# Sixteen experts, latent attention and gated attention of two transformer blocks: weight splits, tile order and pools

## The chip, the core and the metric

The kernel runs on one core of one Trainium2 chip. It has TensorE (PE: matrix products and transposes), VectorE (DVE), ScalarE (ACT), GpSimd (POOL) and a queue that issues transfers (SP); 16 DMA engines move data between memory and the core's on-chip buffer. Each engine runs its own instructions in order and waits for the others by semaphores. The metric is the time of one execution in device microseconds (us), the median of several runs.

## What is computed

Two blocks run one after the other on 1024 tokens of width 1024, all in fp32. The first has four mixers (latent attention, a pooling mixer, a state-space mixer, a gated recurrence), a feed-forward layer and an embedding layer. The second has gated linear attention and retention, then sixteen experts, each of which picks 128 tokens. The parts that matter here, shortened from the reference:

```python
def mla_mixer(c_q, c_kv, k_r, cos, sin, q_norm, w_uq, kv_norm, w_ukv):     # first block
    q = (rmsnorm(c_q, q_norm) @ w_uq).reshape(b, s, MLA_HEADS, QK_NOPE + QK_ROPE)      # 8 heads, 64 + 32
    q_nope, q_rope = q[..., :QK_NOPE], apply_rope(q[..., QK_NOPE:], cos, sin)
    kv = (rmsnorm(c_kv, kv_norm) @ w_ukv).reshape(b, s, MLA_HEADS, QK_NOPE + V_HEAD)   # 64 + 64
    k_nope, v = kv[..., :QK_NOPE], kv[..., QK_NOPE:]
    k_rope = apply_rope(k_r, cos, sin)                                                  # one for all heads
    # causal softmax of (q_nope k_nope + q_rope k_rope) * 96 ** -0.5, times v

def _token_mixer(...):                                                                  # second block
    # gated linear attention (4 heads, keys of 64) and retention (4 heads), forward and backward
    o_g = _head_rmsnorm(o_gf + _flip(o_gb), gla_norm_w) * jax.nn.silu(gg)
    o_r = _head_layernorm(o_rf + _flip(o_rb), ret_norm_w) * jax.nn.silu(rg)
    out = jnp.concatenate([o_g, o_r], axis=-1) @ w_out

def _expert_choice_ffn(h, w_router, w_gate, w_up, w_down):                              # second block
    aff = jax.nn.softmax((h @ w_router).astype(F32), axis=-1)
    gate, idx = lax.top_k(jnp.swapaxes(aff, 1, 2), cap)                                 # cap = 128
    xe = h[bidx, idx]
    a, u = xe @ w_gate, xe @ w_up                                                       # 1024 -> 1408
    ye = (silu(a) * u) @ w_down * gate[..., None]                                       # 1408 -> 1024
    return jnp.zeros_like(h).at[bidx, idx].add(ye)
```

## The kernel before

**Split matmuls.** Nearly every fp32 matrix product is done as three faster ones. `split` makes of a tensor its rounded high part on ScalarE (`_hi`) and the rest by a subtraction on VectorE (`_lo`); `mm3` then issues hi x hi, hi x lo and lo x hi into one accumulator (L104 to L106). A plain fp32 matmul does without the split and is two instructions in the trace. Accumulators and transposes share eight PSUM banks: `ps_mm` and `ps_ax` hand them out in turn, six and two of them in the expert stage.

**What sets the order.** The code is written as one sequential program; a scheduler of tiles places its instructions on each engine, which then runs its own in that order. Filler work covers the stages with long chains: `queue` holds generators (the gates' projections in the first block, the retention projections in the second) and `fill(n)` takes n pieces of them. `until(name)` takes pieces until one that is named is done. A pool (`tile_pool`) gives its space back when it is closed, so the pool that follows in the same space waits for the last readers of the first, stores among them.

**Latent attention** (`mla`, L507). The latents are held feature-major, split (`m_chi`, `m_clo`: 128 features x 1024 tokens each). For each of four groups of two heads, a loop over eight token tiles computes K and V token-major (`kv_tile`: 6 matmuls of 256 columns), then Q (`q_tile`: 9 matmuls of 192 columns). VectorE, ScalarE and GpSimd scale the rows and add the rotary part to `m_kx` (`rope`, four VectorE instructions); `turn` transposes each tile twice (`m_kt`, L607) into `m_kT` and `m_qT`. Scores, softmax and the product with V follow, with fillers between them.

**Gated attention** (`gla`, L1308) runs for two pairs of heads, each in a pool of its own. `decays` is a chain from a small matmul (`g_pre`) over ScalarE and VectorE to `g_la`; `states` transposes that (`g_ktp`, L1345) and builds the running states. Then come the scores (`g_s`), the outputs (`g_o`) and `head_out`. Ahead of the second pair the main program loads `qk` and `gv` anew.

**head_out** (L1078) normalizes a head's output and multiplies it by its gate (`ho_g`): a VectorE product with the row's factor, then a GpSimd product with the gate (L1094, L1095), then four transposes (`ho_p`, L1099). It serves gated attention and `retention`. The output projection behind retention runs its first accumulators in parts (k 0 to 4, 4 to 7, and the last, which needs retention's last head).

**Experts** (from L1822). `plan` lists the weight pieces in the order of use: gate of the next expert (8 pieces of 1408 columns), down of this one (8 of up to 1536), up of the next (8 of 1408). `begin(n)` starts the loads and splits of the first n pieces, `piece` asks for its own and `AHEAD` more. A piece is `split_piece` (load into `e_raw`, ScalarE conversion to `e_hi` at L1842, VectorE subtraction to `e_lo` at L1843) or `native_piece` (load into `e_nat`, used as plain fp32 at L1870), the latter for k = 3 and 7 of gate and up. The first expert uses plain pieces only (`first_piece`), which land in the buffers of the others. The loop over experts transposes the activations (`turn_act`: eleven transposes `e_at` at L2036, in three groups, each split to `e_ah` and `e_al`), computes the next expert's gate (`wide`), chooses and gathers a later expert's tokens (`choose`, `gather`, `turn_x` with `e_xt` and `e_xl`), computes `down`, and then the next expert's up. Its last VectorE product (L2026) ends the activations `e_act`. `last` adds the last expert's rows and normalizes.

## Time and profile before

| | us |
|---|---|
| median of 3 runs | 3755.38 (3750.97 to 3757.4) |
| profiled run | 3756.49 |
| its span | 3754.8 |
| TensorE busy | 3611.5 (96%) |
| VectorE busy | 2142.3 (57%) |
| ScalarE busy | 1630.4 (43%) |
| GpSimd busy | 575.5 (15%) |
| experts, from the second expert's start of transposes to the last down projection, 2944.0 to 3713.1 | 769.10 |

The page divides the span into 40 slices of about 94 us. An engine that is nearly always busy sets the time; for the others it counts when they make that one wait. The timeline shows the start of an instruction, its duration, and in brackets how long its engine had stood idle and which instruction ended that. Matmuls overlap, so what one of them costs is the time from its start to the next one's start, not its duration. The windows give the busy time of each engine in a stretch, the granted clock of TensorE, the share of time in which the DMA engines were busy and the rate in GB/s.

### The profile page before, as it was taken

The numbers are of one execution on the slowest core, as the hardware profiler recorded it, in microseconds if no ns is written. First come the engines' busy times: TensorE is split into PE (matmuls) and PEld (weight loads), VectorE is DVE, ScalarE is ACT, GpSimd is POOL, SyncE is SP. The second block draws the span as 40 slices with busy tenths as digits, with TensorE's granted clock in tenths as the row PEclk, the third lists the DMA queues.
The fourth block names the chain that finished last, engine by engine and source line by source line (L and its number), as shares of the span: only waits on it lengthen the run. The fifth ranks groups of instructions, "written<-read, shape, count | busy, mean of one in ns | idle before, by whom it ended". The sixth has DMA issues, their size and how long they took to land. (4 is left out here: it accounts for less than half of the span.)

```text
span 3754.8 us, 47815 instructions
## 1 busy us (share of the span) xinstructions
PE 3611.5 (96%) x18388; PEld 2917.8 (78%) x18388; DVE 2142.3 (57%) x3235; ACT 1630.4 (43%) x2393; POOL 575.5 (15%) x644
## 2 busy tenths in 40 slices
PE   8999999999999999999999999999996999999998
PEld 6787787777678788888888788778974677777776
DVE  5435424433556666555435647476544677777776
ACT  7433333333323322222125548445332566665565
POOL 0003311111132100000001201123321000123230
PEclk9999999999999999999999999999997999999999
DMA  4221211221456333233213342313356899999997
GB/s 127 65 63 54 79 52 49 74 65 65 144 193 195 109 97 106 91 100 96 73 45 101 105 116 68 96 56 128 119 195 240 286 353 364 358 341 347 373 348 263
DMA packets 295105, 581.84 MB, mean 155 GB/s; under 512 B 27246, under 2 KB 185036, under 8 KB 294876
## 3 DMA queue, kind: packets, MB, share of 16 engines
q1 hardware_dynamic: 272588, 508.47, 39.3%
q0 software_dynamic: 22288, 70.31, 5.6%
q8 instruction: 145, 2.38, 0.3%
q14 instruction: 84, 0.69, 0.1%
HBM read 512.61 MB, written 66.09 MB: 154 GB/s over the span
## 5 line engine op out<-in xcount | busy, mean ns | idle before, releaser
L104 PE MATMUL mm<-hh_hi,w_hi 128*128 128x512 f32 x1872 | 751.3, 402 | 6.2 <-ACT p_u L336 2.0
L105 PE MATMUL mm<-hh_lo,w_hi 128*128 128x512 f32 x1872 | 737.8, 394 | 0.2 <-DVE hh_lo L96 0.2
L106 PE MATMUL mm<-hh_hi,w_lo 128*128 128x512 f32 x1872 | 736.9, 394 | 0.5 <-DVE w_lo L96 0.5
L1843 DVE TENSOR_TENSOR e_lo<-e_raw,e_hi 128x1408 fp32r<-128x1408 f32 (+1 forms) x308 | 489.0, 1621 | 86.2 <-ACT e_hi L1842 70.8
L96 DVE TENSOR_TENSOR w_lo<-w_raw,w_hi 128x1024 fp32r<-128x1024 f32 (+4 forms) x278 | 352.2, 1283 | 278.2 <-ACT w_hi L94 276.8
L1842 ACT ACTIVATE e_hi<-e_raw 128x1408 fp32r<-128x1408 f32 (+1 forms) x308 | 415.2, 1389 | 124.0 <-PE mm L1868 78.7
L104 PEld LDWEIGHTS mm<-hh_hi,w_hi 128*128 128x128 f32 x1872 | 354.2, 189 | 91.1 <-issue 13.6
L94 ACT ACTIVATE w_hi<-w_raw 128x1024 fp32r<-128x1024 f32 (+4 forms) x278 | 270.4, 995 | 340.6 <-PE mm L105 189.8
L106 PEld LDWEIGHTS mm<-hh_hi,w_lo 128*128 128x128 f32 x1872 | 353.8, 189 | 78.4 <-issue 2.3
L105 PEld LDWEIGHTS mm<-hh_lo,w_hi 128*128 128x128 f32 x1872 | 354.2, 189 | 72.3 <-issue 4.9
L104 PE MATMUL mm<-w_hi,hh_hi 128*128 128x256 f32 (+1 forms) x896 | 291.0, 325 | 0.2 <-ACT w_hi L94 0.2
L105 PE MATMUL mm<-w_lo,hh_hi 128*128 128x256 f32 (+1 forms) x896 | 285.2, 318 | 0.0
L106 PE MATMUL mm<-w_hi,hh_lo 128*128 128x256 f32 (+1 forms) x896 | 283.9, 317 | 0.0
L1868 PE MATMUL mm<-e_hi,e_xl 128*128 128x512 f32 x540 | 203.6, 377 | 0.0
L1867 PE MATMUL mm<-e_lo,e_xh 128*128 128x512 f32 x540 | 202.7, 375 | 0.0
L105 PE MATMUL mm<-w_lo,a_hi 128*128 128x512 f32 x512 | 199.6, 390 | 0.0
L104 PE MATMUL mm<-w_hi,a_hi 128*128 128x512 f32 x512 | 199.6, 390 | 0.0
L106 PE MATMUL mm<-w_hi,a_lo 128*128 128x512 f32 x512 | 199.3, 389 | 0.0
L1866 PE MATMUL mm<-e_hi,e_xh 128*128 128x512 f32 x540 | 198.6, 401 | 0.0
L104 PEld LDWEIGHTS mm<-w_hi,hh_hi 128*128 128x128 f32 x896 | 172.5, 193 | 14.3 <-issue 0.8
L105 PEld LDWEIGHTS mm<-w_lo,hh_hi 128*128 128x128 f32 x896 | 172.7, 193 | 10.4 <-issue 1.0
L106 PEld LDWEIGHTS mm<-w_hi,hh_lo 128*128 128x128 f32 x896 | 172.5, 193 | 10.0
(658 smaller groups left out, 6325.4 us busy)
## 6 DMA issues: line engine op xcount, KB each, us to landing
e_raw<-in_w_exp_down_dram SPq DMA_DIRECT2D x112, 768.0 KB
e_raw<-in_w_exp_gate_dram SPq DMA_DIRECT2D x90, 704.0 KB
e_raw<-in_w_exp_up_dram SPq DMA_DIRECT2D x90, 704.0 KB
w_raw<-in_w_in_dram SPq DMA_DIRECT2D x82, 512.0 KB
w_raw<-in_w_ff_dram SPq DMA_DIRECT2D x64, 512.0 KB
w_raw<-in_w_ada_dram SPq DMA_DIRECT2D x48, 512.0 KB
e_nat<-in_w_exp_up_dram SPq DMA_DIRECT2D x32, 704.0 KB
e_nat<-in_w_exp_gate_dram SPq DMA_DIRECT2D x30, 704.0 KB
```

What stands on the lines that cost most here:

```text
L94: S.activation(hi, src, AF.Copy, scale=1.0 if scale is None else scale)
L96: V.tensor_sub(lo, src, hi.bitcast(F32))
L104: P.matmul(ps, ah, bh, start=start and k == 0, stop=False)
L105: P.matmul(ps, ah, bl, start=False, stop=False)
L106: P.matmul(ps, al, bh, start=False, stop=stop and k == nk - 1)
L1842: S.activation(hi[:, :n], r[:, :n], AF.Copy)
L1843: V.tensor_sub(lo[:, :n], r[:, :n], hi[:, :n].bitcast(F32))
L1866: P.matmul(ps, x[0][:, k], w[0][:, c0:c1], start=k == 0, stop=False)
L1867: P.matmul(ps, x[0][:, k], w[1][:, c0:c1], start=False, stop=False)
L1868: P.matmul(ps, x[1][:, k], w[0][:, c0:c1], start=False, stop=k == last)
```

## The change

**Experts.** Pieces 3 and 7 of gate and up are split like the others, for all experts from the second on; `native_piece` and the plain copies `e_xn` of the tokens are gone. The pools of `e_hi`, `e_lo` and `e_raw` have nine buffers each (7, 7 and 8 before, besides 3 of `e_nat`), and `AHEAD` is 8 in place of 6. The loads of all sixteen pieces of the first expert are issued ahead of the top-k, in program order, and `begin` is called during the first expert's gate too.

**Latent attention.** K and Q are computed feature-major at once, weights as the stationary side and 512 tokens as the moving one: K of two heads in 6 matmuls per half of the tokens, Q of one head in 9. V is computed for four heads at a time. The tables of the rotary angles (`m_trig`) and the rotated key part (`m_kpe`) are made and transposed once, by 16 transposes; the weights of Q are laid out so that rotated rows stand beside plain ones (`parted`). The row factor of Q moves into the softmax (`m_qs`), that of K into a row table (`m_krow`, two plain matmuls). `turn`, `rope` and `m_kx` are gone.

**Gated attention.** Both pairs use one pool. `gla` is a generator; the second pair's load and its first `decays` run from `following`, ahead of the first pair's last `g_o` and `head_out`.

**head_out** does both products in one VectorE instruction per 128 columns. **Retention's end** itself issues the output projection's parts k 0 to 4 and 4 to 7 for four tiles, ahead of the last transposes.

```diff
-    LO_A, N_LO, N_HI, N_RAW, N_NAT = 5, 7, 7, 8, 3
-    NATIVE = (3, 7)
-    AHEAD = 6
+    LO_A, N_LO, N_HI, N_RAW = 7, 9, 9, 9
+    AHEAD = 8
...
-        SP.dma_start(r[:, :n], src)
+        tc.keep_in_program_order(SP.dma_start(r[:, :n], src))
         return r
...
+    firsts = []
+    for which, name in enumerate(("w_exp_gate_2", "w_exp_up_2")):
+        src = I[name][0, 0].rearrange("(p j) n -> p j n", j=KD)
+        firsts += [first_piece(which * KD + k, src[:, k], 1408) for k in range(KD)]
...
-                split(x[0][:, b * 4:b * 4 + 3], x[1][:, b * 4:b * 4 + 3], t)
+                split(x[0][:, b * 4:b * 4 + 4], x[1][:, b * 4:b * 4 + 4], t)
...
-                made.append((native_piece if k in NATIVE else split_piece)(src[:, k], 1408))
+                made.append(split_piece(src[:, k], 1408))
...
-            if e == 0 and which == UP:
-                begin(k)
+            if e == 0:
+                begin(min(k, N_HI + N_LO - 2 * KD) if which == GATE else N_HI + N_LO - 2 * KD + k)
...
+            kT = mp2.tile([128, 2, T], F32, name="m_kT")
+            V.tensor_copy(kT[64:128, 0], kpe[64:128])
+            S.activation(kT[0:64, 1], kpe[0:64], AF.Copy)
...
+            def kv_weights(h0, n, s):
+                r = raw_half(2, n * 64)
+                for j in range(2):
+                    SP.dma_start(r[:, j].rearrange("p (h d) -> p h d", h=n), w_ukv[:, j, h0:h0 + n, s])
+                return parted(2, n * 64, r, [(0, 0, n * 64)])
+
             for hg in range(4):
...
+                w = kv_weights(hg * 2, 2, 0)
+                for h in range(2):
                     p = ps_mm()
...
+                    mm3(p, w, cT, 2, lambda t, k: t[:, k, :], lambda t, k: t[:, 3 + k, H5(h)])
+                    for x in range(2):
+                        r = slice(x * 64, x * 64 + 64)
+                        V.tensor_mul(kT[r, x, H5(h)], p[r], krow[r, H5(h)])
+                    fill(1)
+                if hg % 2 == 0:
+                    w = kv_weights(hg * 2, 4, 1)
+                    vt = mp2.tile([128, NT, 4, 64], F32, name="m_v", bufs=1)
                     for i in range(NT):
...
+                        mm3(p[:, :256], cT, w, 2, lambda t, k: t[:, 3 + k, i * 128:(i + 1) * 128],
+                            lambda t, k: t[:, k, :])
...
+                qT = mp2.tile([128, 2, T], F32, name="m_qT", bufs=1)
+                for h in range(2):
+                    for x in range(2):
+                        p = ps_mm()
+                        mm3(p, w, cT, 3, lambda t, k: t[:, k, x * 128:x * 128 + 128], lambda t, k: t[:, k, H5(h)])
+                        own, com = slice(x * 64, x * 64 + 64), slice(64 - x * 64, 128 - x * 64)
+                        S.activation(qT[own, x, H5(h)], p[own], AF.Copy)
+                        V.tensor_mul(qT[com, x, H5(h)], p[com], trig[com, H5(h)])
+                        fill(2)
+                fill(2 if hg % 2 == 0 else 6)
...
-        V.tensor_mul(n, src, B(st))
-        G.tensor_mul(n, n, gt)
+        for c in range(4):
+            V.scalar_tensor_tensor(n[:, c], src[:, c], st[:, c:c + 1], gt[:, c], op0=OP.mult, op1=OP.mult)
...
+            if h == 1:
+                following()
+            until("gg")
...
+                if h == 3:
+                    begun = [ps_mm() for _ in range(4)]
+                    for k0, k1 in ((0, 4), (4, 7)):
+                        for i in range(4):
+                            out_part(begun[i], oT[0], ahead, i, k0, k1)
...
-    nc = bacc.Bacc("TRN2", target_bir_lowering=False, num_devices=1)
+    nc = bacc.Bacc("TRN2", target_bir_lowering=False, num_devices=1, dynamic_dma_scratch_size=4096)
```

What the scheduler makes of it is shown at three places. In these listings a row is one instruction (or several like it, x n), with its line, what it writes and what it reads.

TensorE, at the end of a middle expert's gate matmuls (`e_hi`, `e_lo` with `e_xh`, `e_xl`: the gate), before:

```order
L1868 MATMUL mm<-e_hi,e_xl 128x384
L2036 MATMUL e_at<-ident,e_act 128x128 x8
L1866 MATMUL mm<-e_hi,e_xh 128x512
L1867 MATMUL mm<-e_lo,e_xh 128x512
L1868 MATMUL mm<-e_hi,e_xl 128x512
L1866 MATMUL mm<-e_hi,e_xh 128x512
L1867 MATMUL mm<-e_lo,e_xh 128x512
L1868 MATMUL mm<-e_hi,e_xl 128x512
L2036 MATMUL e_at<-ident,e_act 128x128 x3
L1866 MATMUL mm<-e_hi,e_xh 128x384
```

and after:

```order
L1904 MATMUL mm<-e_lo,e_xh 128x384
L1905 MATMUL mm<-e_hi,e_xl 128x384
L2077 MATMUL e_at<-ident,e_act 128x128 x8
L1903 MATMUL mm<-e_hi,e_ah 128x512
L1904 MATMUL mm<-e_lo,e_ah 128x512
L1903 MATMUL mm<-e_hi,e_ah 128x512
L1904 MATMUL mm<-e_lo,e_ah 128x512
L2077 MATMUL e_at<-ident,e_act 128x128 x3
L1905 MATMUL mm<-e_hi,e_al 128x512 x2
```

The transposes of the activations have moved from among the gate matmuls to right ahead of the down projection (`e_ah`, `e_al`), which reads what they make.

VectorE, at the same place (`e_lo` 1408 wide: gate and up pieces, 1536 wide: down pieces), before:

```order
L1843 TENSOR_TENSOR e_lo<-e_raw,e_hi 128x1408 x8
L2026 TENSOR_TENSOR e_act<-e_act,mm 128x512 x2
L2026 TENSOR_TENSOR e_act<-e_act,mm 128x384
L1843 TENSOR_TENSOR e_lo<-e_raw,e_hi 128x1408
L96 TENSOR_TENSOR e_al<-e_at,e_ah 128x512 x2
L1843 TENSOR_TENSOR e_lo<-e_raw,e_hi 128x1536
L96 TENSOR_TENSOR e_al<-e_at,e_ah 128x384
```

and after:

```order
L1887 TENSOR_TENSOR e_lo<-e_raw,e_hi 128x1408 x11
L2067 TENSOR_TENSOR e_act<-e_act,mm 128x512 x2
L2067 TENSOR_TENSOR e_act<-e_act,mm 128x384
L1887 TENSOR_TENSOR e_lo<-e_raw,e_hi 128x1536 x2
L96 TENSOR_TENSOR e_al<-e_at,e_ah 128x512 x2
L1887 TENSOR_TENSOR e_lo<-e_raw,e_hi 128x1536
L96 TENSOR_TENSOR e_al<-e_at,e_ah 128x384
```

All gate pieces and two down pieces now stand ahead of the instruction that waits for the transposed activations; before, it was all gate pieces and none of the down pieces.

VectorE, from the first pair's last `head_out` to the second pair's first `g_la`, before:

```order
L1094 TENSOR_TENSOR ho_n<-g_o,ho_s 128x512
L1092 TENSOR_REDUCE ho_s<-ho_q 128x4
L110 RECIPROCAL ho_s<-ho_s 128x4
L1094 TENSOR_TENSOR ho_n<-g_o,ho_s 128x512
L96 TENSOR_TENSOR w_lo<-w_raw,w_hi 128x1024 x2
L1365 COPY g_st_18874<-stg 128x128
L1365 COPY g_st_18875<-stg 128x128
L1325 TENSOR_SCALAR g_la<-g_pre,nw 128x512 x2
L1328 TENSOR_TENSOR g_la<-g_la,ho_q 128x512 x2
```

and after:

```order
L1354 TENSOR_SCALAR g_la<-g_pre,nw 128x512
L1357 TENSOR_TENSOR g_la<-g_la,ho_q 128x512
L1360 SCALAR_TENSOR_TENSOR g_cum_18079<-g_rst,g_la 128x512
L1121 TENSOR_REDUCE ho_s<-ho_q 128x4
L1366 TENSOR_TENSOR g_la<-g_cum_18079 128x512
L110 RECIPROCAL ho_s<-ho_s 128x4
L1124 SCALAR_TENSOR_TENSOR ho_n<-g_o,ho_s,ho_g 128x128 x4
L1368 TENSOR_TENSOR g_la<-g_la,g_qk 128x512
```

The chain to the second pair's `g_la` has moved ahead of the first pair's last outputs, and the two copies of the states behind it.

## Rows read from the trace of the kernel before

**Rows 1.** the page: busy us (share of the span) xinstructions; bandwidth in 40 slices

```profile
PE 3611.5 (96%) x18388; PEld 2917.8 (78%) x18388; DVE 2142.3 (57%) x3235; ACT 1630.4 (43%) x2393; POOL 575.5 (15%) x644
...
GB/s 127 65 63 54 79 52 49 74 65 65 144 193 195 109 97 106 91 100 96 73 45 101 105 116 68 96 56 128 119 195 240 286 353 364 358 341 347 373 348 263
```

**Rows 2.** experts: busy PE, PEld, DVE, ACT, POOL; clock, DMA share, GB/s

```profile
2944.00:3713.10 769.10, 755.45 (x3356) 584.68 (x3355) 577.96 (x500) 493.35 (x531) 143.07 (x28) 1.00 0.94 353
3094.40:3145.90 51.50, 51.50 (x234) 40.40 (x234) 39.31 (x35) 33.88 (x36) 3.69 (x2) 1.00 0.96 368
3356.00:3408.30 52.30, 50.97 (x227) 38.88 (x226) 38.32 (x34) 32.59 (x36) 15.48 (x2) 1.00 0.91 346
```

**Rows 3.** timeline, all engines, ahead of the last expert's transposes

```profile
3704.43 1.48 ACT L1842 ACTIVATE e_hi<-e_raw 128x1536 fp32r<-128x1536 f32 x1 [1.30 <-DMA e_raw<-in_w_exp_down_dram]
...
3711.32 1.98 PE L2036 MATMUL e_at<-ident,e_act 128*128 128x128 f32 x8 [6.09 <-DVE e_act L2026]
```

**Rows 4.** timeline, all engines, at the transposes of an expert's activations

```profile
3356.03 1.12 PE L2036 MATMUL e_at<-ident,e_act 128*128 128x128 f32 x8
3356.71 1.09 ACT L94 ACTIVATE e_ah<-e_at 128x512 fp32r<-128x512 f32 x2 [13.80 <-PE e_at L2036]
...
3356.91 0.48 PE L1867 MATMUL mm<-e_lo,e_xh 128*128 128x512 f32 x1
...
3357.34 1.29 DVE L96 TENSOR_TENSOR e_al<-e_at,e_ah 128x512 fp32r<-128x512 f32 x2 [10.89 <-ACT e_ah L94]
```

**Rows 5.** waits: who waits for whom, us in total, times, longest us

```profile
DVE e_al L96 <- ACT e_ah L94: 94.4, 15, 10.9
...
ACT e_hi L1842 <- DMA e_raw<-in_w_exp_gate_dram: 24.0, 34, 3.2
...
PE ho_p L1099 <- POOL ho_n L1095: 8.2, 6, 2.1
```

**Rows 6.** timeline, TensorE: start us, busy us, one native piece between split ones

```profile
3100.52 2.52 PE L1870 MATMUL mm<-e_nat,e_xn 128*128 128x512 f32 x6
3102.59 0.69 PE L1866 MATMUL mm<-e_hi,e_xh 128*128 128x512 f32 x1
...
3104.80 0.40 PE L1866 MATMUL mm<-e_hi,e_xh 128*128 128x512 f32 x1
...
3106.72 0.40 PE L1866 MATMUL mm<-e_hi,e_xh 128*128 128x512 f32 x1
```

**Rows 7.** groups by shape: what xcount | busy us, mean ns | idle us

```profile
L1843 DVE TENSOR_TENSOR e_lo<-e_raw,e_hi 128x1408 fp32r<-128x1408 f32 x180 | 284.0, 1620 | 40.9 <-ACT e_hi L1842 26.0 <-PE mm L1870 14.0 <-DMA e_raw<-in_w_exp_gate_dram 0.6
...
L1870 PE MATMUL mm<-e_nat,e_xn 128*128 128x512 f32 x240 | 112.7, 592 | 0.0
...
L1095 POOL TENSOR_TENSOR ho_n<-ho_n,ho_g 128x512 f32<-128x512 f32 x16 | 22.3, 1394 | 39.5 <-DVE ho_n L1094 23.2 <-DVE ho_s L110 13.3 <-issue 1.8
```

**Rows 8.** timeline, TensorE, latent attention: a K/V tile, then a Q tile

```profile
533.86 0.38 PE L607 MATMUL m_kt<-ident,m_kx 128*96 128x128 f32 x2
533.99 0.36 PE L104 MATMUL mm<-w_hi,m_chi 128*128 128x256 f32 x1
...
534.78 0.40 PE L104 MATMUL mm<-hh_hi,w_hi 128*128 128x512 f32 x1
...
551.86 0.34 PE L104 MATMUL mm<-w_hi,m_chi 128*128 128x192 f32 x1
...
552.92 0.41 PE L104 MATMUL mm<-hh_hi,w_hi 128*128 128x512 f32 x1
...
554.77 0.40 PE L106 MATMUL mm<-hh_hi,w_lo 128*128 128x512 f32 x1
```

**Rows 9.** busy time by engine, DMA share: latent attention with its fillers

```profile
520.00:960.00 440.00, 436.32 (x2555) 340.53 (x2555) 166.86 (x440) 162.83 (x366) 48.13 (x104) 1.00 0.21 66
```

**Rows 10.** timeline, all engines, start of the second pair of gated attention

```profile
2427.50 1.27 ACT L1324 ACTIVATE ho_q<-g_pre,nw 128x512 f32<-128x512 f32 x2 [6.60 <-DMA o<-ho_y]
...
2439.19 1.12 PE L1345 MATMUL g_ktp<-ident,g_la 128*128 128x128 f32 x4 [6.34 <-DVE g_la L1339]
```

More of the change, by code (lines that the diff above doesn't have):

```diff
@@ L570, in mla @@
             rstd_of(rs[:, 1], p[:, 8:16], 256)
+            qs = mp.tile([128, 2, NT], F32, name="m_qs")
+            V.tensor_scalar(qs[:, 0], rs[:, 0], scale, None, op0=OP.mult)
+            V.tensor_scalar(qs[:, 1], rs[:, 0], -scale, None, op0=OP.mult)
+            krow = mp.tile([128, T], F32, name="m_krow")
+            for h in range(2):
+                p = ps_ax("m_krp")
+                P.matmul(p, ones, ss[:, 1, H5(h)], start=True, stop=True)
+                rstd_of(krow[:, H5(h)], p, 256)
             nst.close()
@@ new lines, in states @@
+        def states(d, h, la):
+            p = ps_ax("g_ktp")
+            for i in range(4):
+                P.transpose(p[:, i * 128:(i + 1) * 128], la[:, i * 128:(i + 1) * 128], ident)
+            kt = g2.tile([128, 4, 128], F32, name="ho_y", bufs=1)
+            S.activation(kt.rearrange("p c k -> p (c k)"), p, AF.Copy)
+            order = [0, 1, 2, 3] if d == 0 else [3, 2, 1, 0]
+            for b in (0, 2):
+                p = ps_ax("g_ct")
+                for j, c in enumerate(order[b:b + 2]):
+                    P.matmul(p[:, j * 256:(j + 1) * 256], kt[:, c], gv[:, h * 4 + c], start=True, stop=True)
+                for j, c in enumerate(order[b:b + 2]):
+                    cc = h * 4 + c
+                    nx = cc + 1 if d == 0 else cc - 1
+                    if 0 <= nx < NT:
@@ L1433, in gla @@
-                for o in ho:
-                    next(o)
-                    fill(1)
+                            V.scalar_tensor_tensor(st[d][r, nx], st[d][r, cc], dec[r, d, cc:cc + 1],
+                                                   p[r, j * 256 + x * 128:j * 256 + (x + 1) * 128],
+                                                   op0=OP.mult, op1=OP.add)
+                fill(1)
+        steps = [(0, 0), (0, 1), (1, 1), (1, 0)]
+        la = decays(*steps[0])
+        yield
+        st = [g2.tile([128, NT, 128], F32, name=f"g_st{d}") for d in range(2)]
@@ L1571, in retention @@
                     x, sc, st = nx, nsc, nst
-        return oT, ahead
+        return oT, ahead, begun
     pj = ExitStack()
@@ L1632, in emit, with second @@
         queue.append(projections(pjp, cosT, sinT))
-        gla(0, qk, gv, gz, gconst)
-        until("gla1")
-        for n in range(2):
-            SP.dma_start(qk[:, n], GQK[n])
-        SP.dma_start(gv, rows(GV))
-        gla(1, qk, gv, gz, gconst)
-    oT, ahead = retention()
+        with tc.tile_pool(name="gla2", bufs=1) as g2:
+            pair = [None, None]
+            def second():
+                until("gla1")
+                for n in range(2):
+                    SP.dma_start(qk[:, n], GQK[n])
+                pair[1] = gla(1, qk, gv, gz, gconst, g2, lambda: None)
+                next(pair[1])
+            pair[0] = gla(0, qk, gv, gz, gconst, g2, second)
+            now(pair[0])
+            SP.dma_start(gv, rows(GV))
+            now(pair[1])
+    oT, ahead, begun = retention()
     pj.close()
```

352 lines of the change are left out of this document (157 added, 195 removed).

## Prediction, made before the changed kernel ran

> **What bounds the kernel now.** I read the page's busy shares first: TensorE works 3611.5 us of the 3754.8 us span, and every other engine stands far below it [rows 1]. So an edit counts only where it shortens TensorE's own stream of instructions or one of its few gaps, and I went through the four stages touched with that question. The experts take a fifth of the span: from the first transposes of an expert's activations at 2944.0 to the last expert's first down-projection matmul at 3713.1 lie 769.10 us for fifteen experts, 51.3 us each, of which TensorE is busy 755.45, or 50.4 us per expert [rows 2]. The missing 13.65 us are one gap of 6.09 us ahead of the last expert's transposes [rows 3] and about 7.6 us of small stalls. VectorE is busy 577.96 us there (38.5 per expert), ScalarE 493.35 (32.9), and the DMA engines 0.94 of the time at 353 GB/s. DMA is therefore the resource closest behind TensorE. VectorE has slack, but a forced one: it stands still up to 10.9 us per expert, waiting for the transposed activations [rows 4, 5].
>
> The profiled run took 3756.49 us, 1.1 us over the median of 3755.38. The sum is made against 3756.49.
>
> **Experts: the native pieces.** Sixty weight pieces (k = 3 and 7 of gate and up, experts 1 to 15) go from plain fp32 to the split form. In the trace one native piece runs from 3100.52 to 3102.59, and the split piece behind it pays for the switch: it takes 2.21 us (3102.59 to 3104.80) where the next takes 1.92 (3104.80 to 3106.72) [rows 6]. Native is thus 2.07 + 0.29 = 2.36 us against 1.92, a gain of 0.44 us a piece, 1.76 per expert, 26.4 us in all, and all of it on TensorE's path. The Trainium skill ("FP8 and Floating Point Precision", TensorE Precision Notes) says that true fp32 makes four passes through the array. The split form makes three matmuls, so by that rule a native piece would cost 4/3 of 1.92, or 2.56 us, and the gain would be 38 us; the row says 26, and the row is used, since a native piece changes its weights less often.
>
> What pays for it is VectorE and ScalarE. Each expert adds four subtractions e_lo of 1408 columns at 1.62 us [rows 7], so VectorE goes from 38.5 to 45.0 us per expert; ScalarE adds four conversions of about the same size and goes from 32.9 to some 39. Both remain under the 49 to 50 us worked out below, so TensorE hides them; if a forced pause on VectorE of more than about 5 us remained, they would no longer be hidden (the third rival).
>
> **Experts: the order.** The order shows a second effect. Before, the transposes e_at stand in the middle of the next expert's gate matmuls; after, they stand behind all of them, directly ahead of the down-projection that needs their result. That costs a new bubble. The trace has its parts: transposes start at 3356.03, matmuls go on at 3356.91 in the old order, ScalarE begins e_ah at 3356.71 and VectorE its e_al at 3357.34 [rows 4]. The new order's first down matmul needs e_ah, which is there when e_al starts; so it starts about 0.4 us later than the transposes end. The four matmuls that follow (about 0.9 us) cover e_al. I take +0.4 us per expert; its bounds are 0 (another instruction fills it) and 1.3 us (the second e_al is waited for). In exchange VectorE has all eight gate pieces and two down pieces split before it must wait for e_al. I expect most of the 10.9 us pause and the stalls from late e_lo to go.
>
> So TensorE needs 50.4 - 1.76 + 0.4 = 49.0 us per expert. An expert moves 346 GB/s x 52.3 us = 18.1 MB [rows 2]. At 49.0 us that is 369 GB/s, and with a share of 0.91 for 346 GB/s it means a share of 0.97 to 0.98. The 368 GB/s of the earlier expert (share 0.96) and the 373 GB/s of the best slice [rows 1, 2] say that this can be had, but with little room; ScalarE waits on gate weights 34 times already [rows 5]. I charge 0.6 us per expert for it. The final gap of 6.1 us stays: there the last down pieces come late by DMA [rows 3], and the new order even places all eight of their splits ahead of the last activation. Sum: 15 x 49.6 + 6.1 = 750, against 769: **-19 us**. Bounds: 15 x 49.0 = 735 (-34, no waits at all) and 769 (0, DMA holds the old pace).
>
> The first expert keeps its plain pieces. Their loads go out ahead of the top-k with three more buffers to land in. Neither the count nor the order of the first expert's matmuls changes, so I count nothing. The larger pools and the smaller descriptor scratch cost no instruction of TensorE.
>
> **Latent attention.** Before, each of 32 K/V tiles is 6 matmuls of 256 columns, 0.79 us (533.99 to 534.78), plus its two transposes, 0.13 us (533.86 to 533.99); each of 32 Q tiles is 9 of 192 columns, 1.06 us (551.86 to 552.92), plus two transposes taken at the same 0.13 us [rows 8]. Together 29.4 + 38.1 = 67.5 us. After, K is 48 matmuls and Q 144, all 512 wide; a 512-wide one takes 0.23 us (eight steps in 1.85 us from 552.92 to 554.77), giving 11.0 + 33.1 us. V is 16 tiles of the old 0.79 us, 12.6 us. New are 16 transposes for the angle tables at 0.11 us (eight from 3356.03 to 3356.91 [rows 4]), 1.8 us, and two fp32 matmuls of two instructions each, at most 0.59 us an instruction [rows 7], 2.4 us. Sum 60.9: **-7 us**. The gain is from the transposes and the narrow K/V tiles; Q gains little, because its 192 useful rows per two heads are computed as 256. The bound on the good side is -11, if the 3.7 us that TensorE is idle in this stage (440.00 less 436.32 [rows 9]) go too; on the bad side -1, if TensorE waits once per head group for the rearranged weights (four head groups, about 1.5 us each, the duration of one split). The K weights now come in rows of 256 bytes; with a DMA share of 0.21 in this stage [rows 9] their slowness is hidden by the prefetch, unless the buffers of raw weights run out. The shorter copies and rotations leave ScalarE, VectorE and GpSimd, which are under half busy there, and count nothing.
>
> **Gated attention.** The second pair's first decays wait for the old pool's stores: ScalarE is idle 6.60 us on the DMA of ho_y and then starts, at 2427.50, the chain that ends in g_la; TensorE is idle 6.34 us ahead of g_ktp at 2439.19 [rows 10]. The change emits this pair's load and first decays ahead of the first pair's last outputs, in the same pool. The chain of some 12 us then runs beside matmuls: **-6 us**. If it were only half covered, -3. Next in line are the stores of the outputs, on which nothing of TensorE waits.
>
> **head_out and the end of retention.** TensorE waits 8.2 us in six places for GpSimd's product ho_n [rows 5], which takes 1.39 us each time [rows 7]. Four VectorE instructions of a quarter width now do both products. They cost VectorE more than its one product (perhaps 1 us), but GpSimd's leg is gone. At the last pair 41 more output-projection matmuls (about 9 us) stand ahead of the waiting transposes. I take **-6 us**, with bounds -8 and -2.
>
> **Sum:** -19 - 7 - 6 - 6 = -38, so 3756.5 - 38 = 3718 us.
>
> **Rivals.** (1) *DMA becomes the bound of the experts.* An expert's 18.1 MB at the stage's average of 353 GB/s are 51.3 us, exactly today's pace; then only the other terms stay, and the time is about 3737 us. For it: ScalarE's waits on gate weights, and raw buffers down from eleven (eight and three) to nine. Against it: 368 GB/s in the expert from 3094.4, without a gap on TensorE. The Trainium skill ("DMA: Bandwidth & Descriptors", Specifications) names a limit of about 358 GB/s for one core's share of memory; by it an expert could not be faster than 50.6 us, the experts would gain 10 us and the time would be 3727. The rows of 368 and 373 GB/s lie above that figure. Chance 0.20.
> (2) *Everything is hidden.* No bubble worth the name, no waits for weights, no final gap: experts -34, the other terms at their better ends of -9, -6 and -8: about 3699 us. Chance 0.20.
> (3) *Slower: VectorE becomes the bound.* If its pause for e_al stayed at 10.9 us while its work grows to 45.0, an expert would take 55.9 us instead of 51.3: +69 us, less the 19 of the other parts, about 3806 us. It decides from the point where work and pause exceed 51.3 us, so a pause above 6.3 us. Against it: the pause ends with the transposes, and VectorE comes to it later in the new order. Chance 0.06.
> (4) *The reordering does not do what it says:* the stalls of the middle stages stay (12 us back), and the experts gain at most a little against DMA: about 3748 us, within the 0.2% (7.5 us) that a measurement of this kernel can tell from no change. Chance 0.06.
>
> **How the numbers follow.** The forecast has 0.48, with an own range of 3705 to 3730. The range of 3694 to 3743 takes in rivals 1 and 2 and leaves out rivals 3 and 4, 0.12, and the tails of the others. Faster by over 0.2% are the forecast and rivals 1 and 2: 0.88; the same is rival 4, 0.06; slower is rival 3, 0.06.
>
> **What the new profile should show.** Per expert 49 to 50 us; the DMA share in the experts at 0.96 or more; VectorE busy about 45 us per expert, with a pause for e_al of under 6 us; a gap of about 0.4 us between e_at and the first down matmul; no 6 us gap ahead of the second pair's first g_ktp; at most two waits for ho_n. I would be wrong if the period stayed at 51 us with a DMA share near 1 (rival 1), if VectorE had hardly a pause and TensorE waited for e_lo or e_al (rival 3), or if new gaps showed up in latent attention at the start of head groups.

## The result and the profile after

The changed kernel takes 3712.86 us (median of 4 runs, 3702.58 to 3714.41) against 3756.39 us for the kernel before in the same comparison (4 runs). The ratio is 0.9883, with a 95% interval of 0.9871 to 0.9895: 39 to 48 us faster. In the later comparisons the kernel before had medians of 3749.7 to 3752.7 us; against those medians it is 37 to 40 us faster. The forecast was 3718 us, the range 3694 to 3743. The profiled run took 3714.41 us, its span is 3712.6.

The page of the changed kernel, busy times and bandwidth slices:

```profile
PE 3574.9 (96%) x18268; PEld 2939.4 (79%) x18268; DVE 2238.1 (60%) x3217; ACT 1694.2 (46%) x2384; POOL 667.2 (18%) x596
...
GB/s 128 66 63 51 73 46 66 72 71 55 153 192 184 121 97 98 105 93 93 78 49 107 77 145 62 89 76 78 142 199 238 240 384 345 370 382 377 382 369 253
```

TensorE lost 36.6 us of busy time against [rows 1], and the best bandwidth slice rose from 373 to 384 GB/s. By the marks of the two traces the 42 us of the profiled runs divide as follows. Up to gated attention's first matmul (`g_pre`), which latent attention lies ahead of: -8. From there to the routing's `q_at`, behind retention, which I call the middle stretch: -7. From there to the first token transposes of the first expert: +2.7. From there to the last down projection (e_xt and e_ah first and last, the two views below): -30.

The instructions on e_ah (the down projections) and e_xt (token transposes) with their first and last start, kernel before:

```profile
L1867 PE MATMUL mm<-e_lo,e_ah x352: 387/389/628, 2961.8 to 3729.8; 128*128 128x512 f32 x176
```
```profile
L1961 PE MATMUL e_xt<-ident,e_x x128: 270/276/451, 2900.9 to 3623.6; 128*128 128x128 f32 x128
```

The same of the changed kernel:

```profile
L1904 PE MATMUL mm<-e_lo,e_ah x352: 387/389/628, 2948.0 to 3687.6; 128*128 128x512 f32 x176
```
```profile
L2002 PE MATMUL e_xt<-ident,e_x x128: 270/274/450, 2888.5 to 3582.5; 128*128 128x128 f32 x128
```

From 2900.9 to 3729.8 were 828.9 us; from 2888.5 to 3687.6 are 799.1. These stage figures carry some 3 us of scatter: in the six traces of this study that keep the old latent attention, its first matmul starts between 519.1 and 522.5 us, though no edit touches what stands ahead of it. The ratios are formed from undisturbed runs alone and paired on one chip, so they can differ a little from the quotient of the medians.

The experts in the windows of the changed kernel, the first row from its first e_at to just ahead of the last expert's first down matmul, the second a single expert (us; busy PE, PEld, DVE, ACT, POOL; clock, DMA share, GB/s):

```profile
2933.46:3669.45 735.99, 723.77 (x3526) 615.23 (x3524) 661.64 (x558) 568.88 (x590) 262.91 (x28) 0.99 0.99 370
3235.50:3284.30 48.80, 48.60 (x239) 41.21 (x239) 44.37 (x38) 38.06 (x40) 23.52 (x2) 1.00 0.99 377
```

These answer [rows 2]. An expert in the middle of the stage takes 48.7 to 48.8 us where such a one took 52.3, TensorE stands still 0.2 us in it, VectorE works 44.4 us and the DMA engines are busy 0.99 of the time. The average over the fifteen, without the final gap, went from 50.9 us ((769.10 - 6.09) / 15) to 48.4 ((735.99 - 10.20) / 15). The fifteen stretches from one expert's transposes to the next one's do not hold the same work: the last has no gate of a next expert, and the third to fifth of the changed kernel take 51 to 53 us with up to 262 instructions of TensorE, where the one shown has 239.

The transposes of a middle expert and the last expert's, timeline of all engines of the changed kernel:

```profile
3332.96 1.12 PE L2077 MATMUL e_at<-ident,e_act 128*128 128x128 f32 x8
3333.64 1.09 ACT L94 ACTIVATE e_ah<-e_at 128x512 fp32r<-128x512 f32 x2 [8.49 <-PE e_at L2077]
3334.27 1.29 DVE L96 TENSOR_TENSOR e_al<-e_at,e_ah 128x512 fp32r<-128x512 f32 x2 [2.75 <-ACT e_ah L94]
...
3334.29 0.50 PE L1903 MATMUL mm<-e_hi,e_ah 128*128 128x512 f32 x1 [0.20 <-ACT e_ah L94]
```
```profile
3667.81 1.99 PE L2077 MATMUL e_at<-ident,e_act 128*128 128x128 f32 x8 [10.20 <-DVE e_act L2067]
```

Against [rows 4], VectorE's pause for e_al has gone from 10.89 to 2.75 us. The first down matmul starts 1.33 us after the transposes begin, where 0.88 would do without a wait: a bubble of 0.45 us. Against [rows 3], the gap ahead of the last expert's transposes has grown from 6.09 to 10.20 us.

TensorE's waits of the changed kernel (who for whom, total us, times, longest):

```profile
PE e_at L2077 <- DVE e_act L2067: 10.2, 1, 10.2
PE e_xt L2002 <- DMA e_x<-h2d,idx: 8.1, 1, 8.1
...
PE g_ktp L1374 <- DVE g_la L1368: 4.5, 2, 2.7
...
PE r_s L1554 <- DMA r_v<-rv: 3.2, 1, 3.2
...
PE g_o L1455 <- DVE g_sc L1438: 2.9, 1, 2.9
...
PE r_kt L1528 <- DVE r_sc L1555: 2.1, 1, 2.1
```

The 6.34 us gap ahead of the second pair's g_ktp [rows 10] and the 8.2 us on ho_n [rows 5] are gone. In their place stand waits that were shorter or not there: that of r_s on the load r_v, g_sc and r_sc.

### The profile page after: what moved, and what is told of

Read it like the earlier page. It is cut to its first block, busy times and chain, and to the rows that moved or that the text cites. A ratio compares the mean times of both kernels' runs of the same rounds, so it can differ in the third digit from the quotient of the medians.

```text
span 3712.6 us, 47408 instructions
## 1 busy us (share of the span) xinstructions
PE 3574.9 (96%) x18268; PEld 2939.4 (79%) x18268; DVE 2238.1 (60%) x3217; ACT 1694.2 (46%) x2384; POOL 667.2 (18%) x596
## 5 line engine op out<-in xcount | busy, mean ns | idle before, releaser
L1887 DVE TENSOR_TENSOR e_lo<-e_raw,e_hi 128x1408 fp32r<-128x1408 f32 (+1 forms) x368 | 579.1, 1618 | 42.5 <-ACT e_hi L1886 37.8
L96 DVE TENSOR_TENSOR w_lo<-w_raw,w_hi 128x1024 fp32r<-128x1024 f32 (+5 forms) x296 | 350.0, 1202 | 304.4 <-ACT w_hi L94 300.3
L1886 ACT ACTIVATE e_hi<-e_raw 128x1408 fp32r<-128x1408 f32 (+1 forms) x368 | 492.6, 1390 | 77.6 <-PE mm L1905 41.9
L94 ACT ACTIVATE w_hi<-w_raw 128x1024 fp32r<-128x1024 f32 (+5 forms) x296 | 272.9, 948 | 355.0 <-PE mm L105 199.8
L1905 PE MATMUL mm<-e_hi,e_xl 128*128 128x512 f32 x720 | 270.6, 376 | 0.0
L1904 PE MATMUL mm<-e_lo,e_xh 128*128 128x512 f32 x720 | 268.9, 373 | 0.0
L2095 POOL DMA_INDIRECT xacc<-e_y,idx x15 | 227.7, 15183 | 226.8 <-DVE e_y L2092 226.8
L1903 PE MATMUL mm<-e_hi,e_xh 128*128 128x512 f32 x720 | 239.6, 377 | 0.0
```

What stands on the lines that cost most here:

```text
L94: S.activation(hi, src, AF.Copy, scale=1.0 if scale is None else scale)
L96: V.tensor_sub(lo, src, hi.bitcast(F32))
L1886: S.activation(hi[:, :n], r[:, :n], AF.Copy)
L1887: V.tensor_sub(lo[:, :n], r[:, :n], hi[:, :n].bitcast(F32))
L1903: P.matmul(ps, x[0][:, k], w[0][:, c0:c1], start=k == 0, stop=False)
L1904: P.matmul(ps, x[0][:, k], w[1][:, c0:c1], start=False, stop=False)
```

## The experiments

My theory after the result: in the experts TensorE's own work sets the time, the split saves it, and the order (eight pieces begun ahead) removes the stalls. Its rival: the depth alone, or the DMA rate, decides. For the other two parts the question was whether they are worth what the traces show.

### One part alone

**e1_experts.** The expert hunks of the change on the kernel before (with the smaller scratch).

> The kernel before with the expert part alone (and the smaller descriptor scratch that makes room for its pools); latent attention, gated attention, head_out and the end of retention as before. Theory A (the parts add up, each worth what the marks in the two traces give): from the first token transposes to the last down projection 29.8 us less, the gather ahead of it 2.7 us later, so about 27 us faster, 3729 us. Theory B (the parts lean on each other: the experts gain only because the stages ahead hand over earlier): under 20 us.

Measured 3725.70 us against 3752.21, ratio 0.9928 (0.9911 to 0.9944): 27 us faster, as theory A has it. TensorE's wait for the first gather of tokens, 5.1 us before, is 7.6 us in this kernel:

```profile
PE e_xt L1956 <- DMA e_x<-h2d,idx: 7.6, 1, 7.6
```

So it is the experts' own part that lengthens that wait; which of its loads do, e8_tail_gather shows.

**e2_split.**

```diff
-    LO_A, N_LO, N_HI, N_RAW = 7, 9, 9, 9
-    AHEAD = 8
+    LO_A, N_LO, N_HI, N_RAW = 6, 8, 8, 8
+    AHEAD = 6
...
-                w = firsts[which * KD + k]
+                w = first_piece(which * KD + k, matrix(which, e)[:, k], 1408)
```

> The kernel before, with the native pieces split like the others, pools of eight, six pieces begun ahead as before, and the first expert's loads where they were. Theory A (the gain of the experts is TensorE's own work, 0.44 us a piece for 60 pieces, 26 us): 22 to 28 us faster, about 3731 us, with an expert every 49 to 50 us. Theory B (the gain is the depth: nine buffers and eight ahead remove the pauses): under 10 us, since VectorE gets 6.5 us more work per expert and keeps its pause for e_al of some 10 us.

Measured 3740.32 us, ratio 0.9966 (0.9954 to 0.9979): 13 us faster. Neither theory: half of what the split should give. Seven experts of this kernel in the windows, with VectorE's pause and TensorE's wait on e_lo in the same stretch:

```profile
3250.00:3600.00 350.00, 342.27 (x1630) 282.32 (x1629) 306.57 (x260) 263.16 (x276) 139.35 (x14) 1.00 0.98 364
```
```profile
DVE e_al L96 <- ACT e_ah L94: 24.2, 6, 4.1
...
PE mm L1858 <- DVE e_lo L1841: 6.3, 13, 0.8
...
PEld mm L1858 <- DVE e_lo L1841: 15.4, 25, 1.2
```

The same stretch of the changed kernel:

```profile
3250.00:3600.00 350.00, 348.57 (x1693) 295.58 (x1692) 316.14 (x268) 274.48 (x288) 144.22 (x14) 1.00 1.00 378
```

In the same 350 us TensorE runs 1630 instructions here and 1693 there; an expert takes 50.7 us against 48.7. In the order of this kernel, with the old depth, VectorE comes to e_al before it has any down piece split, and TensorE then waits some 0.9 us per expert for the e_lo of the down pieces. That is half of the 2 us. The rest shows in the weight loads: they wait 15.4 us for e_lo in these 350 us, some 2.2 us an expert, where those of the changed kernel wait for none. Part of that stands as busy time of TensorE, 0.210 us an instruction (342.27 / 1630) against 0.206 (348.57 / 1693), about 1 us in the 236 instructions of an expert.

**e3_pools.**

```diff
-    LO_A, N_LO, N_HI, N_RAW, N_NAT = 5, 7, 7, 8, 3
+    LO_A, N_LO, N_HI, N_RAW, N_NAT = 6, 8, 8, 8, 3
...
-    AHEAD = 6
+    AHEAD = 8
```

> The kernel before, pieces 3 and 7 still native, with pools of eight for e_hi and e_lo and eight pieces begun ahead. Theory A: at most the 7.6 us of small stalls on e_lo and e_al can go, so 0 to 8 us faster, 3748 to 3756. Theory B: 15 us or more, 3741 or less.

Measured 3751.75 us, ratio 1.0000 (0.9990 to 1.0009). Depth without the split is worth nothing that can be told. The split without depth is worth 13, both together 27: the two belong together.

**e4_middle.** The hunks of gated attention, head_out and retention's end on the kernel before.

> The kernel before with gated attention in one pool, head_out on VectorE and the begun output projection; experts and latent attention as before. The prediction put 12 us on this (6 and 6): 3744 us. The two traces show that the waits of 6.3 us ahead of g_ktp and of 8 us on ho_n are gone, yet this stretch is only 7 us shorter, because others grew (the load of r_v 1.4 to 3.2 us, g_sc 1.7 to 2.9, w_hi behind the begun projection 1.7, q_xT 0.8 to 2.2): by that theory 3749 us, 7 us faster.

Measured 3751.31 us, ratio 0.9997 (0.9987 to 1.0007): 1 us, with an interval from 5 faster to 3 slower. By these times the 12 us of the prediction are excluded, 7 are too. Its trace says a little more: the middle stretch is 595.0 us, against 598.8 before.

**e9_latent.** The hunks of latent attention (and the smaller scratch, which makes room for its tables) on the kernel before.

> The kernel before with the feature-major latent attention alone (and the smaller descriptor scratch, which leaves room for its tables). Theory A (the prediction's sum of matmuls): 7 us less work on TensorE; against the profile of the experts-alone run, in which this stage is the old one, the mark behind the stage comes 4.6 us earlier and 8.6 us net of what the stage ahead happened to take: 4 to 9 us faster, 3743 to 3748 us. Theory B (what is left of the whole change's 44 us when the experts' 27 and the middle's 1 are taken off): 14 us or more, 3738 us or less; then the parts are worth more together than apart.

Measured 3745.48 us against 3752.56, ratio 0.9983 (0.9974 to 0.9992): 6 to 7 us faster, theory A. Two groups of its matmuls (busy us, mean ns | idle before):

```profile
L104 PE MATMUL mm<-m_chi,w_hi 128*128 128x512 f32 x64 | 26.1, 408 | 0.0
...
L104 PE MATMUL mm<-w_hi,m_chi 128*128 128x256 f32 x32 | 9.6, 301 | 4.2 <-ACT g_sig L757 2.3 <-DVE m_kT L624 1.9
```

The counts are those of the sum (3 x 64 of 512 columns, 3 x 32 of 256). The 512-wide ones wait for nothing; V waits 4.2 us in all, put down to ScalarE's g_sig (2.3) and VectorE's m_kT (1.9), which both read accumulators. The sum did not have that.

**e12_gated.** Gated attention in one pool alone.

> The kernel before with gated attention in one pool alone; head_out and the end of retention as before. Theory A (the wait of 6.3 us ahead of g_ktp goes, and the waits that grew in the run with the whole middle part belong to the other edits, which moved retention's end): 5 to 6 us faster, 3746 us, with the wait for r_v still at 1.4 us. Theory B (the gain is given back in the same stage, where the second pair's g_ct, g_sc and then r_v are waited for longer): 0 to 3 us, with waits for g_sc of 2.9 us and for r_v of 3 to 4 us.

Measured 3748.45 us against 3752.56, ratio 1.0002 (0.9991 to 1.0012): no difference that the times can tell, though its ten runs lie far apart (3747.65 to 3764.47). TensorE's waits in its stretch:

```profile
PE r_s L1525 <- DMA r_kT<-rqk: 3.2, 1, 3.2
PE g_o L1426 <- DVE g_sc L1409: 3.1, 1, 3.1
PE r_kt L1499 <- DVE r_sc L1526: 2.0, 1, 2.0
```

In the kernel before the wait of g_o was 1.7 us, that of r_s 1.4, and r_kt had none. These three appear with the one pool alone, without head_out or the begun projection: the chain that no longer delays g_ktp lets TensorE arrive earlier at the next things that come from VectorE and from memory. The waits and the times are those of theory B. The middle stretch of its trace is not: 592.1 us against 598.8 before, the 6 us of theory A. Times and trace disagree here; the stretches of the other traces, below, side with the trace.

### The changed kernel with one thing altered

**e6_ahead6.** `AHEAD = 6` in place of 8.

> The changed kernel with six pieces begun ahead in place of eight, the pools of nine kept. The run with split pieces and the old depth gave 13 us where the whole expert part gave 27. Theory A (the depth in the code, AHEAD, decides where the transposes stand and so when VectorE may go on): about 12 us slower than the changed kernel, an expert every 50 to 51 us. Theory B (the number of buffers decides, since the scheduler fills whatever is free): within 3 us of the changed kernel, 48.7 us an expert.

Measured 3726.90 us, ratio 0.9924 (0.9908 to 0.9941) against 0.9883: about 15 us slower than the changed kernel, theory A. The waits in seven experts of this kernel (3250 to 3600 us) show the picture of e2_split, a pause of 4.1 us and waits on e_lo:

```profile
DVE e_al L96 <- ACT e_ah L94: 28.2, 7, 4.1
...
PE mm L1904 <- DVE e_lo L1887: 6.3, 14, 0.7
```

**e11_pools8.** Pools of eight (`LO_A, N_LO, N_HI, N_RAW = 6, 8, 8, 8`), AHEAD 8.

> The changed kernel with pools of eight for e_hi, e_lo and e_raw in place of nine, eight pieces still begun ahead; the order of TensorE's instructions round e_at stays the new one. Theory A (the depth in the code decides, through the order): within 4 us of the changed kernel. Theory B (the ninth buffer is needed to keep the transfers going): 48.7 us an expert become 50 or more, 15 us slower or more.

Measured 3710.64 us, ratio 0.9894 (0.9879 to 0.9909): the changed kernel's time within the interval, 48.7 us an expert. The ninth buffer does nothing for the time; how many pieces stand ahead in the program does. That number sets the depth and the order at once, and no run parts the two.

**e7_vector_load.**

```diff
-        V.tensor_sub(lo[:, :n], r[:, :n], hi[:, :n].bitcast(F32))
+        for _ in range(2 if twice else 1):
+            V.tensor_sub(lo[:, :n], r[:, :n], hi[:, :n].bitcast(F32))
...
-                made.append(split_piece(src[:, k], 1408))
+                made.append(split_piece(src[:, k], 1408, k in (1, 5)))
```

> The changed kernel with four subtractions e_lo per expert (k = 1 and 5 of gate and up) done twice, the output unchanged: VectorE gets 6.5 us more per expert, as much again as the change gave it, from 44.3 to 50.8 us. Theory A (TensorE bounds the experts at 48.7 us and VectorE has some 4 us to spare, nearly all of it usable): VectorE becomes the bound at 51 to 51.5 us an expert, 30 to 42 us slower than the changed kernel. Theory B (the pause for e_al stays a forced one, as in the prediction's slower rival): 53.5 us or more an expert, over 70 us slower.

Measured 3748.34 us, ratio 0.9983 (0.9973 to 0.9993) against 0.9883: 37 us slower than the changed kernel, within theory A's 30 to 42.

Seven experts of this kernel in the windows, and the waits of TensorE and VectorE there:

```profile
3250.00:3600.00 350.00, 329.20 (x1551) 275.24 (x1551) 335.08 (x277) 256.31 (x267) 62.88 (x14) 0.98 0.96 348
```
```profile
PE mm L1905 <- DVE e_lo L1888: 19.8, 10, 3.0
...
DVE e_al L96 <- ACT e_ah L94: 5.6, 6, 1.7
```

VectorE is busy 335 of 350 us and its pause has shrunk to under 1 us per expert; now TensorE waits for e_lo. So VectorE does become the bound: 50.9 us of work exceed TensorE's 48.7 by 2.2 us, and 37 us over fifteen experts are 2.5 each. Its pause is not a fixed price on top. The experts in the window are slower than that average, some 53 us (1551 instructions where the changed kernel runs 1693), of which VectorE works 50.9 and stands idle 2.3; the profiled run was the slowest of ten.

**e10_bytes.**

```diff
-        SP.dma_start(r[:, :n], src)
+        SP.dma_start(r[:, :loaded or n], src)
...
+                wide_ = src.rearrange("p j n -> p (j n)")[:, k * 1408:k * 1408 + 1536] if k < 7 else src[:, k]
+                made.append(split_piece(wide_, 1408, 1536 if k < 7 else 1408))
```

> The changed kernel with 1536 instead of 1408 columns loaded for 14 of the 16 gate and up pieces of an expert; the extra columns are never read and nothing else changes. An expert moves 0.9 MB more, 19.0 instead of 18.1. Theory A (the DMA share of 1.00 at 376 GB/s in the experts is a ceiling): 19.0 MB take 50.5 us, so 1.8 us more per expert, some 25 us slower than the changed kernel, with waits of ScalarE on e_raw in every expert. Theory B (TensorE alone bounds them; 401 to 417 GB/s, as in the quiet stretches, can be had): within 4 us of the changed kernel, 48.7 us an expert.

Measured 3712.92 us, ratio 0.9895 (0.9880 to 0.9910) against 0.9883: theory B, within 4 to 5 us.

The same stretch of this kernel in the windows:

```profile
3250.00:3600.00 350.00, 348.56 (x1694) 295.56 (x1693) 317.16 (x270) 274.91 (x288) 154.10 (x14) 1.00 1.01 396
```

396 GB/s over 350 us, with TensorE as busy as in the changed kernel (348.57 us, 378 GB/s, share 1.00). A share of 1.00 was no ceiling. The added bytes came as longer rows, so the run does not show what the same number of bytes in more rows would cost, nor where the ceiling lies.

**e8_tail_gather.** Two mends on the changed kernel: the last expert's down pieces are begun at most two ahead of its activations, and the first nine loads for later experts go out on GpSimd's queue, behind the first gather.

```diff
-        begin(n + 1 + AHEAD)
+        begin(min(n + 1 + AHEAD, len(plan) - 6) if (which, e) == (UP, 15) else n + 1 + AHEAD)
...
+        if len(made) < N_RAW:
+            tc.keep_in_program_order(G.dma_start(r[:, :n], src))
+        else:
+            SP.dma_start(r[:, :n], src)
...
+        if e < 1:
+            tc.keep_in_program_order(x)
```

> The changed kernel with two places mended that its trace shows. At the end at most two of the last expert's down pieces are begun ahead of its activations, so that VectorE's last product does not queue behind splits that wait for transfers (TensorE idle 10.2 us there). At the start the first nine pieces for the later experts are loaded from GpSimd's queue behind the first gather of tokens, so that the gather does not queue behind them (8.1 us idle). Theory A (both waits are queueing): the first falls to 4 to 6 us, the second to 3 us, 9 to 11 us faster than the changed kernel. Theory B (the end is bound by the last weights' arrival and the gather by its own latency): under 3 us faster.

Measured 3696.68 us against 3752.66, ratio 0.9850 (0.9834 to 0.9867): 12 us faster than the changed kernel by the two ratios, a little more than theory A, and the fastest version of this study. The last expert's transposes in the timeline of this kernel, and TensorE's wait for the first gather:

```profile
3648.20 1.25 PE L2082 MATMUL e_at<-ident,e_act 128*128 128x128 f32 x8 [1.26 <-DVE e_act L2072]
...
3652.14 0.63 PE L2082 MATMUL e_at<-ident,e_act 128*128 128x128 f32 x3 [1.30 <-DVE e_al L96]
```
```profile
PE e_xt L2007 <- DMA e_x<-h2d,idx: 4.8, 1, 4.8
```

In the timeline and in the waits 10.2 us have become 1.26 and 1.30, and 8.1 have become 4.8. The end was queueing, but not on transfers, as I had expected. VectorE at the end of the changed kernel, then its last product in this one:

```profile
3644.52 21.57 DVE L1887 TENSOR_TENSOR e_lo<-e_raw,e_hi 128x1408 fp32r<-128x1408 f32 x14
...
3666.01 1.74 DVE L2067 TENSOR_TENSOR e_act<-e_act,mm 128x512 f32<-128x512 f32 x3
```
```profile
3646.40 1.74 DVE L2072 TENSOR_TENSOR e_act<-e_act,mm 128x512 f32<-128x512 f32 x3
```

In the changed kernel VectorE works through fourteen splits without a pause and only then comes to its last product; it waits for no transfer there, although ScalarE does (6.1 us in four places). Here eight splits stand ahead of that product (12.6 us). So the product stood behind VectorE's own work. Of the gather's wait only 3.3 us were queueing, behind the nine loads for later experts that this kernel moves; 4.8 remain with the DMA engines idle ahead of it (a share of 0.02 or less from 2866 to 2874 us).

**e13_no_middle.** The changed kernel without its middle part.

> The changed kernel without its middle: gated attention in two pools, head_out and the end of retention as before; experts and latent attention as changed. The parts alone gave 27 (experts), 6 to 7 (latent attention) and 1 us (middle), 34 to 35 together; the whole gave 40 to 44 against before. Theory A (the parts add up and the rest is scatter between builds): 33 to 34 us faster than before, 3719 us. Theory B (the middle is worth 6 to 9 us in the company of the others, as its stretch in the changed kernel's profile says, 592 us against 598): the same 33 to 34 us here, so A and B agree on this run if the other two add up; then the difference to the changed kernel is the middle's worth. Theory C (latent attention is worth more beside the new experts): 38 us or more, 3714 us or less, and the middle stays at about 1 us.

Measured 3721.06 us against 3749.67, ratio 0.9923 (0.9910 to 0.9937): 29 us faster than before (24 to 34), which the 33 to 34 of A and B just reach. The difference to the whole (0.9883) puts the middle at some 15 us in this company, with an interval of about 8 to 22, where alone it was 1. The middle stretch of this kernel's trace is 601.4 us, that of the whole 591.7. The times of the parts do not close; what the traces add is below.

## Why the prediction was right, step by step

**What bounds the kernel:** right. TensorE is at 96% of the span before and after, and an expert runs at TensorE's pace (348.57 of 350 us busy).

**The total.** 38 us were forecast and 42 lie between the two traces: experts and gather 27 where 19 were forecast, latent attention's stretch 8 where 7, the middle 7 where 12. That the misses of 8 and 5 us nearly cancel is luck.

**Experts, -19 predicted, 27 measured alone.** The mechanism held and one term was mis-sized. In the stretch that the prediction summed, 769.10 us became 735.99, so 33 us where 19 were forecast and 34 were the best bound. TensorE's time per expert was put at 49.0 us, an average of the fifteen, and that average came out at 48.4, 9 us in all. The bubble ahead of the down projection was put at 0.4 us and is 0.45. The pause for e_al was to fall under 6 us and fell to 2.75. What failed is the 0.6 us per expert, 9 us in all, that I charged for DMA near saturation: TensorE waits for no weight at all in the steady experts, and e10_bytes shows that 5% more bytes would have been carried too. A share near 1.00, which I took for little room, is no limit: 346 GB/s at 0.91 would make 380 GB/s at 1.00, and e10_bytes ran at 396. Smaller misses went the other way. The final gap was to stay at 6.1 us and grew to 10.2. The prediction put the old gap down to late transfers, but VectorE's idle time ahead of its last product was only 1.7 us of it (0.65 and 1.03, on e_hi). It did see that the order places all eight last splits ahead of the last activation, and gave that no price; e8_tail_gather shows that this queueing cost 7 to 8 us. With 9 us less for DMA, 9 less for TensorE and 4 more for the gap the sum is the measured -33. Outside the stretch, where the prediction counted nothing, 6 us were lost: 2.7 ahead of the first expert, because more loads stand ahead of its gather, 1.9 in the first expert (43.1 to 45.0 us, cause not traced) and 1.5 behind the last gap (16.7 to 18.2 us). That leaves the 27.

**Split and order.** The prediction added the split (26 us) and the order's removal of stalls as if they were separate. e2_split and e6_ahead6 show that they are not: the split pays its 26 us only if VectorE has down pieces ready when the transposes come, since the split itself raises VectorE's work from 38.5 to 44 us per expert. Half of the gain hangs on the number 8. By an estimate from the four passes that the Trainium skill ("FP8 and Floating Point Precision", TensorE Precision Notes) gives true fp32, the split would have saved 0.64 us a piece and made an expert 50.4 - 2.6 + 0.45 = 48.3 us. With the row's 0.44 us it is 49.1. The measured average is 48.4, but this does not decide for the four passes: the kernel before had such hidden waits on e_lo as well (its weight loads wait 9.9 us for e_lo from 3250 to 3600 us, those of the changed kernel not at all), and their end lowers the average too.

**Latent attention, -7 predicted, 6 to 7 measured (e9_latent).** Right, by the counts and the price per matmul. TensorE's waits for the weights (w_hi) in that stage are 0.9 us in e9_latent, 1.2 us before, so the 256-byte rows are hidden.

**Gated attention and head_out, -6 and -6 predicted; for both together 1 us by the time of e4_middle (at most 5), about 7 by the traces.** This is the step that failed. Both waits vanished as described, 14 us of them, but about half of that came back. The sentence "Next in line are the stores of the outputs, on which nothing of TensorE waits" was wrong: next in line were g_sc (1.7 to 2.9 us), retention's first scores r_s (1.4 us, put down to ScalarE, to 3.2, put down to a load) and r_sc (new, 2.1 us), and e12_gated has all three with gated attention's edit alone. Its middle stretch of 592.1 us is also as short as that of the whole, so the traces show nothing that head_out and retention's end add; neither was run alone. In the middle of the kernel TensorE waits at several chains one after the other, and a wait that is removed is partly paid at the next.

**What stays open.** The parts alone sum to 27 + 7 + 1 = 35 us (27 to 42 with their intervals), the whole gave 44 in its own comparison (39 to 48), and the whole without its middle 29. The intervals overlap, and the stretches that no edit touches differ by up to 4 us from one build's trace to another's. The kept traces say more of the middle, each by one execution (the middle stretch, us):

| middle | kernels | stretch |
|---|---|---|
| old | before, e1, e2, e3, e9, e13 | 598.8, 599.1, 598.2, 598.4, 597.7, 601.4 |
| gated attention alone | e12 | 592.1 |
| new | e4, the changed kernel, e6, e7, e8, e10, e11 | 595.0, 591.7, 591.0, 593.1, 589.6, 594.3, 589.5 |

The old and the new do not overlap, and their means are 7 us apart. With 7 for the middle the parts sum to 41. The times of 1 us (e4_middle) and 15 us (e13_no_middle) lie on either side of it; that scatter in other stretches made them so is likely and not shown. A small interplay of the middle with the rest is not excluded: alone its stretch is 3 to 6 us shorter than the old ones, in company 10 us shorter than that of e13_no_middle.

**Rivals.** The DMA bound (rival 1) is excluded by e10_bytes: 396 GB/s were moved for 350 us without a longer expert. The Trainium skill ("DMA: Bandwidth & Descriptors", Specifications) gives about 358 GB/s as one core's share of memory. Here, with one core at work, that share was no limit. VectorE as the bound (rival 3) exists, but its threshold lies between VectorE's 44.4 us of work in the changed kernel and the 50.9 us of e7_vector_load, and by the latter's 2.5 us per expert near TensorE's own 48.7. Rival 2's experts came true inside their stretch (33 of 34 us) and were given back in part outside it; of rival 4 the returning stalls came true by half. Two details of the recorded text are off without touching its sum: rival 2 takes -9 for latent attention where the bound above it is -11, and the buffers that the first expert's pieces land in grew from 17 to 18, not by three.

## What to carry to other kernels

When work is moved from the busiest engine to another, price the order along with it: here the split was worth 13 us without deeper prefetch, the prefetch nothing without the split, and both 27. Before counting a removed wait as a gain, look up the next-longest wait on the same engine in the same stage: only the difference is sure. An in-order engine at the end of a loop deserves its own look, since work begun ahead for the next step can stand in front of the result that everyone waits for.

## What the runs showed of the hardware

The DMA engines' busy share is not a measure of what is left: at a share of 1.00 the experts moved 378 GB/s, and at 1.01, with longer rows, 396 GB/s, without a wait of TensorE for a weight in either.

After the 10.2 us gap at the end of the changed kernel TensorE's granted clock was at its lower level, 1.2 GHz. Its windows there (us; busy PE, PEld, DVE, ACT, POOL; clock, DMA share, GB/s):

```profile
3660.00:3665.00 5.00, 0.00 (x0) 0.00 (x0) 5.00 (x4) 3.48 (x3) 0.00 (x0) 0.55 1.02 399
3665.00:3670.00 5.00, 2.19 (x9) 1.96 (x10) 3.15 (x6) 0.77 (x2) 0.00 (x0) 0.50 1.02 409
```

The eight transposes there take 1.99 us against 1.12 in a middle expert, so a gap costs more than its own length. In e8_tail_gather, where the gap is 1.26 us and the granted clock stays at 1.00, the same eight take 1.25 us. In the kernel before they took 1.98 us behind 6.09 us of gap [rows 3], with the clock at 0.50 as well.
